# All 64-column products of a pair of experts in one block, all whole-array work in another

## The chip, the cores and the metric

The kernel runs on one core of one Trainium2 chip. The metric is the time of one execution on the device in microseconds (us), the median of several runs.

## What is computed

The kernel is one layer of a decoder trunk for 512 tokens of 1024 features: a norm, four token mixers, an output projection, a second norm, then a mixture of 32 experts of which each token uses two. The change touches the experts alone:

```python
def expert_block(args):
    xe, e = args
    return (jax.nn.silu(xe @ w1[e]) * (xe @ w3[e])) @ w2[e]

yb = lax.map(expert_block, (xb, blk_expert)).reshape(P, D)
yb = yb * row_gate[:, None].astype(yb.dtype)
out = jax.ops.segment_sum(yb, row_tok, num_segments=T + 1)[:T]
```

`w1` and `w3` of an expert are 1024 x 512, `w2` is 512 x 1024, all in float32. The result is multiplied by a vector `g2` and added to `x`.

## The kernel before

Everything up to the router is as before the change and fills the first 819 us. Then the 32 experts are done in 16 pairs. Each expert has 64 slots for its tokens, so a pair has 128; what an expert has beyond 64 tokens is done in a loop of its own, `overflow` (L1396), entered once, at pair 5 (`OVP`).

The work of one pair `p`, and the names that stand for it in the rows:

- `front`: `ph`, the pair's 128 slots against `w1` and `w3`. The two experts' products are 64 columns of the array each and run side by side, so a matrix product there is a tile of 128 x 64. A load brings 512 rows of one matrix; the four parts (two of `w1`, two of `w3`) are 16 instructions each. Then a sigmoid on ScalarE (L1316), a multiplication on VectorE (L1317) and the gating (L1349) give `g`.
- the tables: `pq` (the slots' gates, 4 small products, then L1338 to L1344 on VectorE) and `pr` (four transposes at L1334, copied to `pT` by ScalarE).
- `Back.turn`: four transposes of `g` into `gTp` (L1361), copied to `gT` by ScalarE (L1363).
- `Back.product(n)`: `py`, half `n` of the columns of `gT` times `w2`, again 64 columns of the array per expert, 16 instructions; then `py` times `g2` on VectorE (L1374), `yh` on ScalarE (L158) and `yl` on VectorE (L159), the two parts in which a float32 number goes through the faster product.
- `Back.add(n)`: `po`, `pT` times `yh` and `yl` for each of four blocks of tokens, on the whole array, added to `xm` on VectorE (L1386).
- `group`: every second pair, the rows of 0 and 1 (`pg`, L1097 to L1099 on VectorE) of the next four experts' 256 slots, and `xeps`, 64 whole-array products that gather their tokens, in two halves, one read by ScalarE and one by VectorE (L1480) into `xe`.

All products are issued by `mm` at L60, so one line stands for most of TensorE's work and the names tell it apart. From the router on TensorE's order is the order of the program (a manual schedule); the other engines' order is set by a scheduler.

`front` is a generator that stops behind each of its four parts, and the loop over pairs puts other work into the stops: the additions of the pair before last behind the first and second part, the tables behind the first, `turn` of the pair before behind the third. So 64-column and whole-array products alternate. The second product of pair `p - 1` comes behind `front(p)`. In an odd pair a half of the gather stands ahead of each half of it.

In PSUM `po`, `pr`, `pq` and, up to pair 13, `py` take turns in three buffers of one pool (`psm`); `ph`, `xeps` and the last pairs' `py` take turns in two buffers of twice the size (`psz`). Each half of a product asks for a buffer of its own.

The weights come through SyncE's queue in a fixed list `order`, 198 loads (L1068), into a ring of 18 tiles, each as soon as its tile is free. `w2` of pair `p - 1` stands behind `w1` and `w3` of pair `p` in that list, which is the order of use. At most 76 loads (`most`) are issued ahead of the overflow loop.

Of the kernel before, what the change touches and what calls it, by code (L numbers as in the profile page):

```python
# [39 lines left out]
def trunk(ctx, tc, x, c, ada_w, ada_b, norm1_g, norm2_g, w_in, hgrn_lb, hgrn_norm_g, conv_w, conv_b, conv_ln_g,  # L40
# [7 lines left out]
    def sigmoids(*pairs):  # L48
        """one after the other on ScalarE once all are ready; it otherwise has the table set of exp and ln."""
        with tc.manual_schedule(engines=ACT):  # L50
            if len(pairs) > 1:
                for n, (_, i) in enumerate(pairs):
                    A.activation(tick[:, 2 * n:2 * n + 2], i[:, i.shape[1] - 2:, i.shape[2] - 1] if len(i.shape) == 3 else i[:, 510:512], AF.Copy)
            with tc.high_priority():
                for o, i in pairs:
                    A.activation(o, i, AF.Sigmoid)
                A.preload_act_table_set(LNEXP)
# [20 lines left out]
    # ---- pools of the first part  # L78
# [9 lines left out]
    # ---- loads that everything waits for: c, norm1_g, the first of ada_b; x  # L88
# [7 lines left out]
    # ---- constants  # L96
# [26 lines left out]
    # silu(c) in columns  # L123
# [11 lines left out]
    # ---- x: rms over the row, then transposed  # L135
# [3 lines left out]
    def rsqrt(dst, sums, scale, gain=1.0):  # L139
        """gain / sqrt(sums * scale + EPS), a few columns: exp(-ln / 2) and one Newton step."""  # L140
# [15 lines left out]
    def split(h_ap, l_ap, src):  # L156
        """src = h + l, each of 12 bits."""
        A.activation(h_ap, src, AF.Copy)  # L158
        V.tensor_sub(l_ap, src, h_ap.bitcast(F32))  # L159
# [3 lines left out]
    def ada_load(hf, tiles):  # L163
        """columns hf of 2 of the first two parts of ada_w."""
# [5 lines left out]
    def ada_sum(hf, ps, k):  # L170
        """sh1 and sc1 = silu(c) ada_w (+ ada_b); each quarter on 32 partitions."""
# [12 lines left out]
    def ada_cols(hf, ps):  # L184
        """the sums in columns, into a1 and b1."""
# [40 lines left out]
    def spare(n):  # L226
        """products that nothing needs, so that the array's clock stays up."""
        for _ in range(n):
            mm(scr[:, :128], ident, ident, True, True)
# [12 lines left out]
    # ---- weights: loaded, split in two parts of 12 bits  # L242
# [16 lines left out]
    # ---- the first half of h, the first block's products with it, meanwhile the second half  # L259
# [49 lines left out]
    # ---- masks  # L309
# [29 lines left out]
    def step():  # L339
        """the mixer in hand, as far as its next matrix products; true at its end."""  # L340
# [16 lines left out]
    def three(o, l, r, nk, first=True, last=True):  # L357
        """o += sum over k of (l_h r_h + l_h r_l + l_l r_h); a mixer's products come between."""
# [9 lines left out]
    def fm(w, ci, nk=KD, r=hR):  # L368
        """128 columns of a product, features on partitions."""
# [4 lines left out]
    def tm(w, t, o):  # L374
        """a block's columns of a product, tokens on partitions."""
# [3 lines left out]
    def tm_v(col, nm, tag="d2"):  # L379
        """256 columns, token-major: [128, chunk, 256]."""  # L380
# [22 lines left out]
    def flip(x, nm):  # L403
        """tokens on partitions [128, 4, 256] to features on partitions [128, 2, 512], in PSUM."""
# [6 lines left out]
    def unit(sq, n, gain=1.0):  # L411
        """of squares [128, 1024]: gain / sqrt(mean + EPS) of each n."""
# [6 lines left out]
    # ================= conformer convolution  # L419
# [28 lines left out]
    def conv_ln(res):  # L448
        def over_channels(y, z):
            """a token's sum over the channels / 128, tokens on partitions."""  # L450
# [50 lines left out]
    # ================= HGRN2  # L501
    lbc = mix.tile([128, 4], F32, name="lbc")     # lower bound of the layer: softmax over the layers, cumulated
# [7 lines left out]
    l_a = mix.tile([128, 4], F32, name="l_a")     # max(log(max(lb, 1e-30)), LOG_TINY)  # L510
# [3 lines left out]
    l_c = mix.tile([128, 4], F32, name="l_c")     # log1p(-lb)  # L514
# [20 lines left out]
    def hg_mix(res, hb, f, q, v, g):  # L535
# [22 lines left out]
        # pairs of one position  # L558
# [41 lines left out]
    def linear_out(k, v, am, qd, dec):  # L600
        """o of a linear recurrence, tokens on partitions: in chunks of 128 by am, across them by a state."""
# [29 lines left out]
    def finish(res, o, gcol, hb, g, nm):  # L631
        """head rms, the silu gate; then features on partitions, gain, and split."""
# [17 lines left out]
    # ================= stick breaking  # L650
# [3 lines left out]
    def sb_mix(res, hb, q, k, v):  # L654
# [23 lines left out]
        def scores(p, j):  # L678
            """of a block of 128 keys: log(1 + e^z), and log sigmoid(z); only of the past."""
# [15 lines left out]
        def sums(j, l, lr, start):  # L695
            """et += l sp of a block."""
# [36 lines left out]
    # ================= retention  # L733
# [86 lines left out]
    # ================= the four mixers, the gates and the branch projections  # L820
# [84 lines left out]
    def ada_rest(q, acc_, raws, row=None, before=None):  # L905
        """columns of silu(c) ada_w + ada_b, 1024 of them: on all partitions, or in columns."""
# [31 lines left out]
    def late_sums():  # L938
        """sh2, a2, and g1 once the tables of the retention are done with."""
# [30 lines left out]
    def last_sums():  # L970
        """g1, then g2."""
# [21 lines left out]
    # logits of a token: its x . (a2 wr) over its rms, and sh2 . wr + b  # L993
# [9 lines left out]
    # ================= output projection, second norm, router  # L1003
# [5 lines left out]
    # small tables for the router  # L1009
# [11 lines left out]
    slot = keep.tile([128, 4, NT], F32, name="slot")     # slots and gates of a token's two experts  # L1021
    sg = keep.tile([128, 6, NT], F16, name="sg")         # the same, the gates times 2^15 in two parts of 11 bits
# [7 lines left out]
    # ---- the experts' weights in the order of their use, each tile loaded as soon as there is room  # L1030
# [3 lines left out]
    def cuts(p):  # L1034
        """the columns of a pair's second product, a part at a time; those of the last pair are smaller."""
# [3 lines left out]
    def parts(p, i):  # L1039
        """the rows of a pair's first products, likewise."""  # L1040
# [7 lines left out]
    for p in range(16):  # L1048
# [4 lines left out]
        if 0 < p < 15:  # L1053
            second(p - 1)
        if p > 13:
            second(p)
# [19 lines left out]
    def first_max(v, n, nm, hot=True):  # L1076
        """of v [128, 2, n]: its maxima, the first indices that have them, and those as rows of 0 and 1."""
# [15 lines left out]
    def rows(g, p_, ts):  # L1093
        """the rows of 0 and 1 of 256 slots."""
# [6 lines left out]
    def gather(p_, pv_, ts, ds):  # L1101
        """the slots' tokens, a feature block at a time."""
# [8 lines left out]
    def meanwhile(p_, pv_):  # L1111
        """products for the time in which the second half's experts are found: half of the first gather, in parts,
        and some that nothing needs, so that the array's clock stays up."""
# [19 lines left out]
    def route(half, pl, between=None):  # L1133
        """the experts, ranks in them, and gates of 256 tokens; their rows over their rms, split."""
# [7 lines left out]
        # rows times 2^10, of at most 2^15, in two parts of 11 bits  # L1142
# [43 lines left out]
        # slot of a token in its expert's block of 64; behind that, -1 here  # L1186
# [11 lines left out]
        # gates: softmax of the two, times the group's probability  # L1198
# [71 lines left out]
    def overflow_tables():  # L1270
        """blocks of 128 slots for what an expert has beyond 64 tokens: their number, experts, a token's slot there."""
# [30 lines left out]
    # ================= experts  # L1302
# [4 lines left out]
    def front(p, cur, p_, xe):  # L1307
        """the two experts of a pair: one-hot rows and gates of their slots, silu(x w1) * (x w3) * gate; in parts."""
        so = p % 2 * 128
        ph = psz("ph")  # L1310
        g = None

        def swish():
            nonlocal g
            g = moe.tile([128, 512], F32, name="g", bufs=1)
            A.activation(g, ph[:, 0], AF.Sigmoid)  # L1316
            V.tensor_mul(g, g, ph[:, 0])  # L1317

        for i in range(2):
            if p == 15 and i:  # L1320
                swish()
            for r0, r1 in parts(p, i):
# [5 lines left out]
                yield  # L1328
                if (i, r0) == (0, 512):
                    pr, pq = ps_mm.tile([128, 1024], F16, name="pr", tag="mm"), psm("pq")  # L1330
                    for t in range(NT):
                        mm(pq[:, :6], p_[:, t, so:so + 128], sg[:, :, t], t == 0, t == NT - 1)
                    for t in range(NT):
                        T.transpose(pr[:, t * 128:(t + 1) * 128], p_[:, t, so:so + 128], ident16)  # L1334
                    # the first or the second gate of the token, as it is its first or its second slot
                    ga = moe.tile([128, 4], F32, name="ga")
                    two = pq[:, 2:6].rearrange("p (k a) -> p a k", a=2)
                    V.tensor_scalar(ga[:, 0:1], pid, 128.0 * p, None, op0=OP.add)  # L1338
                    V.tensor_scalar(ga[:, 1:2], pq[:, 0:1], ga[:, 0:1], 2.0 ** -15, op0=OP.is_equal, op1=OP.mult)
                    V.tensor_copy(ga[:, 2:4], two[:, 0])  # L1340
                    V.scalar_tensor_tensor(ga[:, 2:4], two[:, 1], 2.0 ** -11, ga[:, 2:4], op0=OP.mult, op1=OP.add)
                    V.tensor_mul(ga[:, 0:1], ga[:, 1:2], ga[:, 2:3])
                    V.scalar_tensor_tensor(ga[:, 3:4], ga[:, 1:2], 2.0 ** -15, ga[:, 3:4], op0=OP.subtract, op1=OP.mult)
                    V.tensor_sub(ga[:, 0:1], ga[:, 0:1], ga[:, 3:4])  # L1344
                    pT = moe.tile([128, 512], F32R, name="pT")
                    A.activation(pT, pr[:, :512], AF.Copy)
        if p < 15:
            swish()
        V.scalar_tensor_tensor(g, g, ga[:, 0:1], ph[:, 1], op0=OP.mult, op1=OP.mult)  # L1349
        cur[:] = p, g, pT  # L1350

    class Back:
        """a pair's second product, added to its tokens: the parts of the product, then those of the sum."""
# [11 lines left out]
        def product(self, n):  # L1365
            cs = cuts(self.p)[n]
            n_ = cs.stop - cs.start
# [118 lines left out]
    for _ in group(0):  # L1486
        pass
# [68 lines left out]
```

## Time and profile before

| | |
|---|---|
| median of 3 runs | 1319.75 us |
| lowest, highest | 1318.61, 1320.47 us |
| profiled execution: span | 1318.6 us |
| profiled execution: own time | 1318.6 us |
| PE, DVE, ACT busy | 96%, 55%, 35% |
| HBM read, written | 289.68 MB, 2.10 MB |

The span is from the first to the last instruction of the profiled execution. PE is TensorE, PEld its loading of weights, DVE VectorE, ACT ScalarE, SP SyncE. A line number belongs to the kernel before. "128\*64" in a row is the tile of the array. "x16" is the number of instructions in a group or piece. What stands in brackets at the end of a row of the timeline is how long the engine was idle ahead of it, and what it waited for. `PEclk` is the granted clock of TensorE, 1.00 being full speed.

### The profile page before, as it was taken

Reading aid. Unit: us, or ns where it says so; the run is one execution under the profiler, and the core shown is the slowest. Engines: PE = TensorE matmul, PEld = TensorE weight load, DVE = VectorE, ACT = ScalarE, POOL = GpSimd, SP = SyncE. Lnnn points to the kernel's source line nnn. Section 1 sums busy time; section 2 is a strip of 40 time slices with the busy share of each in tenths; the row PEclk is TensorE's granted clock in tenths of the full one; section 3 lists DMA queues with packets and bytes.
Section 4 is the critical chain, followed back from the end, with each engine's and each line's share of the span. In section 5 each row is a group of like instructions: output and inputs, shape, how many; then the busy total and the mean of one; then the engine's idle time right before and its main releaser. Section 6 shows DMA issues by size and latency. Waiting matters only on the chain. (4 is left out here: it accounts for less than half of the span.)

```text
span 1318.6 us, 17997 instructions
## 1 busy us (share of the span) xinstructions
PE 1269.6 (96%) x7265; PEld 881.3 (67%) x7265; DVE 720.7 (55%) x1262; ACT 466.5 (35%) x651; POOL 197.9 (15%) x154
## 2 busy tenths in 40 slices
PE   7999998999999999999999998999989999999997
PEld 5789888987779987787888895444334434343434
DVE  2624679998955464568754565344342444334344
ACT  4447464445454366453334542111101111011111
POOL 3135746101110112121111201000000000000000
PEclk9999997999999999999999998999999999999999
DMA  9422211122222222247782594999989999999997
GB/s 342 140 97 82 79 65 33 50 78 65 96 64 68 94 96 64 81 136 239 248 259 96 196 353 155 385 386 386 387 325 386 387 387 386 387 386 387 386 387 265
DMA packets 177474, 292.98 MB, mean 222 GB/s; under 512 B 8329, under 2 KB 63705, under 8 KB 177389
## 3 DMA queue, kind: packets, MB, share of 16 engines
q1 hardware_dynamic: 174248, 289.45, 61.9%
q10 hardware_dynamic: 2724, 2.26, 0.6%
q8 instruction: 58, 0.95, 0.3%
q14 instruction: 28, 0.22, 0.0%
q0 software_dynamic: 416, 0.10, 0.0%
HBM read 289.68 MB, written 2.10 MB: 221 GB/s over the span
## 5 line engine op out<-in xcount | busy, mean ns | idle before, releaser
L60 PE MATMUL ph<-ew,xe 128*64 128x512 f32 x1024 | 231.8, 597 | 1.4 <-DVE g L1317 1.0
L60 PE MATMUL mm<-hh,wh 128*128 128x512 f32 x448 | 178.9, 399 | 0.0
L60 PE MATMUL mm<-hh,wl 128*128 128x512 f32 x448 | 175.0, 391 | 1.6 <-DVE wl L267 1.6
L255 DVE TENSOR_TENSOR wl<-raw,wh 128x2048 fp32r<-128x2048 f32 x55 | 129.7, 2359 | 83.8 <-ACT wh L254 83.6
L60 PE MATMUL mm<-hl,wh 128*128 128x512 f32 x448 | 174.8, 390 | 0.0
L60 PEld LDWEIGHTS ph<-ew,xe 128*64 128x64 f32 x1024 | 69.5, 137 | 131.3 <-issue 127.8
L254 ACT ACTIVATE wh<-raw 128x2048 fp32r<-128x2048 f32 x55 | 105.2, 1912 | 75.5 <-PE mm L60 75.2
L60 PE MATMUL mm<-wh,hh 128*128 128x256 f32 x448 | 130.4, 291 | 0.0
L60 PE MATMUL mm<-wl,hh 128*128 128x256 f32 x448 | 127.4, 284 | 0.0
L60 PE MATMUL mm<-wh,hl 128*128 128x256 f32 x448 | 127.4, 284 | 0.0
L1386 DVE TENSOR_TENSOR xm<-xm,po 128x512 f32<-128x512 f32 (+1 forms) x136 | 80.4, 651 | 67.7 <-PE po L60 67.7
L60 PE MATMUL py<-ew,gT 128*64 128x512 f32 (+1 forms) x544 | 116.0, 570 | 1.4 <-ACT gT L1363 1.4
L60 PEld LDWEIGHTS mm<-hh,wh 128*128 128x128 f32 x448 | 84.2, 188 | 23.3 <-issue 7.2
L60 PEld LDWEIGHTS mm<-hh,wl 128*128 128x128 f32 x448 | 84.1, 188 | 19.9 <-DVE wl L267 1.9
L60 PEld LDWEIGHTS mm<-hl,wh 128*128 128x128 f32 x448 | 84.2, 188 | 16.6 <-DVE hl L207 0.3
L60 PEld LDWEIGHTS mm<-wh,hh 128*128 128x128 f32 x448 | 86.5, 193 | 6.0 <-issue 5.8
L60 PEld LDWEIGHTS mm<-wl,hh 128*128 128x128 f32 x448 | 86.6, 193 | 0.2
L60 PEld LDWEIGHTS mm<-wh,hl 128*128 128x128 f32 x448 | 86.5, 193 | 0.0
L60 PEld LDWEIGHTS py<-ew,gT 128*64 128x64 f32 x544 | 37.7, 137 | 68.3 <-issue 63.4
L60 PE MATMUL xeps<-pg,xhl 128*128 128x256 f16 x512 | 62.3, 281 | 5.2 <-DVE pg L1099 5.0
L441 DVE SCALAR_TENSOR_TENSOR acc<-z,colB,acc 128x512 f32<-128x512 f32 x90 | 67.2, 789 | 0.0
L60 PEld LDWEIGHTS <-xhl 128*128 128x128 f16 x512 | 50.5, 101 | 23.8 <-issue 16.0
(438 smaller groups left out, 2014.4 us busy)
## 6 DMA issues: line engine op xcount, KB each, us to landing
ew<-in_expert_w_dram SPq DMA_DIRECT2D x186, 1024.0 KB, 14.3
raw<-in_w_in_dram SPq DMA_DIRECT2D x26, 1024.0 KB, 5.0
raw<-in_w_gate_dram SPq DMA_DIRECT2D x16, 1024.0 KB, 5.6
adaw<-in_ada_w_dram SPq DMA_DIRECT2D x64, 256.0 KB, 3.3
aw<-in_ada_w_dram SPq DMA_DIRECT2D x32, 256.0 KB, 5.4
raw<-in_w_branch_dram SPq DMA_DIRECT2D x8, 1024.0 KB, 5.3
raw<-in_w_out_dram SPq DMA_DIRECT2D x6, 1024.0 KB, 6.1
ew<-in_expert_w_dram SPq DMA_DIRECT2D x12, 512.0 KB, 10.0
```

Of the source, the lines that this page charges most:

```text
L60: T.matmul(o, l, r, start=start, stop=stop, skip_group_check=True)
L254: a = A.activation(wh, raw, AF.Copy)
L255: v = V.tensor_sub(wl, raw, wh.bitcast(F32))
L441: V.scalar_tensor_tensor(a, z, cw(k, j), a, op0=OP.mult, op1=OP.add)
L1386: V.tensor_add(xm[:, t, cs], xm[:, t, cs], po)
```

## The change

Three edits, all in the expert phase.

1. `front` is no generator any more. A pair's four parts run one behind the other, `tables` is a function of its own, and the loop over pairs first issues both halves of the second product of the pair before, then all of `front(p)`, and behind it everything on the whole array: the additions, a gather's halves in odd pairs, `turn`, the tables of the next pair. The additions of pair `p - 1` now all come behind `front(p)`; six of the eight stand ahead of `turn` and two behind it. The special order for pairs 14 and 15 is gone.
2. Both halves of a second product of pairs 0 to 14 are one tile `self.py` of the pool with the two large buffers; pair 15 has four parts in tiles of their own as before.
3. The list of loads has `w1`, `w3`, `w2` of each pair, as they are used now.

Comments are gone as well, so line numbers differ.

```diff
-        if 0 < p < 15:
-            second(p - 1)
-        if p > 13:
-            second(p)
+        second(p)
...
-    def front(p, cur, p_, xe):
+    def tables(p, p_):
...
+    def front(p, ga, xe):
         so = p % 2 * 128
         ph = psz("ph")
...
-                yield
-                if (i, r0) == (0, 512):
-                    pr, pq = ps_mm.tile([128, 1024], F16, name="pr", tag="mm"), psm("pq")
...
             cs = cuts(self.p)[n]
+            if self.p < 15 and not n:
+                self.py = psz("py")
             n_ = cs.stop - cs.start
             w = [next(ew), next(ew)]
-            py = (psz("py")[:, 0] if self.p > 13 else psm("py"))[:, :n_]
+            py = psz("py")[:, 0, :n_] if self.p > 14 else self.py[:, n]
...
     for p in range(16):
-        b = Back(*cur) if p else None
-        f = front(p, cur, *gr)
-        gg = group(p // 2 + 1) if p % 2 and p < 15 else iter(())
-        for n, _ in enumerate(f):
-            if b and n == 2 and p < 15:
-                b.turn()
-            if late_ and n < 2:
-                late_.add(0, (2 * n, 2 * n + 1))
-                late_.add(1, (2 * n, 2 * n + 1))
-            if n == 2 and p != OVP:
-                next(gg, None)
+        if b:
+            b.product(0)
+            b.product(1)
+        ga, pT = nxt
+        g = front(p, ga, xe)
         if p == 1:
             eobi, oslot = overflow_tables()
...
+        if p != OVP:
+            next(gg, None)
+        if b:
+            b.add(0)
+        if p != OVP:
+            next(gg, None)
+        if b:
+            b.add(1, (0, 1))
         if p == OVP:
-            for n in range(2):
-                b.product(n)
-            for n in range(2):
-                b.add(n)
+            b.add(1, (2, 3))
             pe_order.close()
...
+        late_, b = b, Back(p, g, pT)
+        b.turn()
+        if late_ and p != OVP:
+            late_.add(1, (2, 3))
...
+        if p < 15:
+            p_, xe = gr
+            nxt = tables(p + 1, p_)
```

How the instructions move, at three places. First TensorE around the second product of an even pair of the later part; `DMAHW..`, `DVE`, `Activation` and `PE` in brackets are the semaphores that an instruction waits for: a load, VectorE, ScalarE, TensorE. Before:

```order
L1361 MATMUL gTp<-ident,g 128x128 x4
L60 MATMUL ph<-ew,xe 64x512 [waits DMAHW5_49]
L60 MATMUL ph<-ew,xe 64x512 [waits DMAHW6_49]
L60 MATMUL ph<-ew,xe 64x512 x6
L60 MATMUL py<-ew,gT 64x512 [waits DMAHW7_49,DVE_49,Activation_49]
L60 MATMUL py<-ew,gT 64x512 [waits DMAHW0_49]
L60 MATMUL py<-ew,gT 64x512 x6
L60 MATMUL py<-ew,gT 64x512 [waits DMAHW1_49,PE_49]
L60 MATMUL py<-ew,gT 64x512 [waits DMAHW2_49]
L60 MATMUL py<-ew,gT 64x512 x6
```

And now:

```order
L60 MATMUL py<-ew,gT 64x512 [waits DMAHW3_49,Activation_49]
L60 MATMUL py<-ew,gT 64x512 [waits DMAHW4_49]
L60 MATMUL py<-ew,gT 64x512 x6
L60 MATMUL py<-ew,gT 64x512 [waits DMAHW5_49,DVE_49]
L60 MATMUL py<-ew,gT 64x512 [waits DMAHW6_49]
L60 MATMUL py<-ew,gT 64x512 x6
L60 MATMUL ph<-ew,xe 64x512 [waits DMAHW7_49,PE_49]
L60 MATMUL ph<-ew,xe 64x512 [waits DMAHW0_49]
L60 MATMUL ph<-ew,xe 64x512 x6
```

`turn` no longer stands between the parts of `ph`; the product comes first and `ph` behind it, and the second half's first product has VectorE among its waits.

Second, TensorE in the whole-array work of an even pair. Before:

```order
L60 MATMUL po<-yh,pT 128x512 [waits DVE_49]
L60 MATMUL po<-yl,pT 128x512
L60 MATMUL ph<-ew,xe 64x512 [waits DMAHW5_49]
L60 MATMUL ph<-ew,xe 64x512 [waits DMAHW6_49]
L60 MATMUL ph<-ew,xe 64x512 x6
L60 MATMUL po<-yh,pT 128x512 [waits DVE_49]
L60 MATMUL po<-yl,pT 128x512
L60 MATMUL po<-yh,pT 128x512 [waits DVE_49]
L60 MATMUL po<-yl,pT 128x512
L60 MATMUL po<-yh,pT 128x512 [waits DVE_49]
L60 MATMUL po<-yl,pT 128x512
```

And now:

```order
L60 MATMUL po<-yh,pT 128x512 [waits DVE_49,Activation_49]
L60 MATMUL po<-yl,pT 128x512
L60 MATMUL po<-yh,pT 128x512 [waits DVE_49]
L60 MATMUL po<-yl,pT 128x512
L1352 MATMUL gTp<-ident,g 128x128 x4
L60 MATMUL po<-yh,pT 128x512 [waits DVE_49]
L60 MATMUL po<-yl,pT 128x512
L60 MATMUL po<-yh,pT 128x512 [waits DVE_49]
L60 MATMUL po<-yl,pT 128x512
L60 LDWEIGHTS pg
L60 MATMUL pq<-sg,pg 128x6 [waits DVE_49]
```

The additions stood in fours on either side of a part of `ph`; now they stand together, with `turn` ahead of the last two and the tables behind them.

Third, VectorE in an even pair, from the gating of `g` to the additions. Before:

```order
L1317 TENSOR_TENSOR g<-g,ph 128x512
L1349 SCALAR_TENSOR_TENSOR g<-g,ga,ph 128x512
L1338 TENSOR_SCALAR ga<-pid 128x1
L1374 TENSOR_TENSOR py<-py,g2b 128x512
L159 TENSOR_TENSOR yl<-py,yh 128x512
L1374 TENSOR_TENSOR py<-py,g2b 128x512
L159 TENSOR_TENSOR yl<-py,yh 128x512
L1386 TENSOR_TENSOR xm<-xm,po 128x512 x8
```

And now, from the split of the product on:

```order
L1367 TENSOR_TENSOR py<-py,g2b 128x512
L159 TENSOR_TENSOR yl<-py,yh 128x512
L1367 TENSOR_TENSOR py<-py,g2b 128x512
L159 TENSOR_TENSOR yl<-py,yh 128x512
L1379 TENSOR_TENSOR xm<-xm,po 128x512
L1339 TENSOR_TENSOR g<-g,ph 128x512
L1379 TENSOR_TENSOR xm<-xm,po 128x512
L1340 SCALAR_TENSOR_TENSOR g<-g,ga,ph 128x512
L1379 TENSOR_TENSOR xm<-xm,po 128x512 x6
L1316 TENSOR_SCALAR ga<-pq,ga 128x1
```

The multiplication and the gating of `g` now stand among the additions, and both halves of the split ahead of all of them.

## Rows read from the trace of the kernel before

**Rows 1.** Page, part 1: busy time, share and instructions of each engine.

```profile
PE 1269.6 (96%) x7265; PEld 881.3 (67%) x7265; DVE 720.7 (55%) x1262; ACT 466.5 (35%) x651; POOL 197.9 (15%) x154
```

**Rows 2.** Stretches: length, busy us of each engine, PEclk, DMA share, GB/s.

```profile
818.90:989.75 170.85, 163.86 (x830) 68.06 (x831) 71.53 (x217) 21.26 (x36) 0.00 (x0) 0.99 0.99 363
989.75:1299.23 309.48, 304.17 (x1554) 131.48 (x1553) 119.09 (x274) 39.50 (x70) 0.00 (x0) 0.99 1.05 385
1299.23:1318.60 19.37, 13.94 (x100) 9.21 (x100) 9.46 (x25) 2.13 (x5) 0.00 (x0) 0.97 0.58 194
```

**Rows 3.** Chain of waits, pairs 6 to 8: start us, us, what.

```profile
1008.96 0.59 PE gTp L1361 x4
...
1020.00 3.43 PE ph L60 x16
1023.44 2.17 PE po L60 x8
1025.60 3.58 PE ph L60 x16
1029.19 0.67 PE po L60 x2
...
1029.88 1.89 DVE xm L1386 x3
...
1031.82 0.38 PE pr L1334 x4
...
1039.96 3.60 PE xeps L60 x32
...
1070.11 0.59 PE gTp L1361 x4
```

**Rows 4.** Timeline, a product's first half: start, us, engine line, out<-in, [idle before].

```profile
1199.82 0.14 PEld L60 LDWEIGHTS py<-ew,gT 128*64 128x64 f32 x2 [0.29 <-issue]
1200.06 0.70 DVE L1374 TENSOR_TENSOR py<-py,g2b 128x512 f32<-128x512 f32 x1 [1.15 <-PE py L60]
...
1200.86 0.60 ACT L158 ACTIVATE yh<-py 128x512 fp32r<-128x512 f32 x1 [3.63 <-DVE py L1374]
...
1201.49 0.69 DVE L159 TENSOR_TENSOR yl<-py,yh 128x512 fp32r<-128x512 f32 x1 [0.72 <-ACT yh L158]
```

**Rows 5.** Timeline of TensorE, pair 15's first products.

```profile
1292.12 2.37 PE L60 MATMUL ph<-ew,xe 128*64 128x512 f32 x10 [1.00 <-DVE g L1317]
```

**Rows 6.** Groups of VectorE, 1000 to 1270 us: count, then busy us, mean ns.

```profile
L1349 DVE SCALAR_TENSOR_TENSOR g<-g,ga,ph 128x512 f32<-128x512 f32 x9 | 6.7, 748 | 0.3
L1317 DVE TENSOR_TENSOR g<-g,ph 128x512 f32<-128x512 f32 x9 | 6.2, 687 | 57.8 <-ACT g L1316 57.8
```

**Rows 7.** Groups of VectorE, 840 to 865 us.

```profile
L1285 DVE TENSOR_SCALAR_CACHE_REDUCE tmp<-ends 128x32 f32<-128x32 f32 x16 | 3.0, 186 | 0.5
```

**Rows 8.** Timeline of VectorE, pair 5's additions; chain of waits behind the overflow loop.

```profile
980.25 3.67 DVE L1386 TENSOR_TENSOR xm<-xm,po 128x512 f32<-128x512 f32 x6
...
989.75 8.18 PE xeps L60 x58
```

**Rows 9.** Chain of waits, the last pair.

```profile
1301.40 3.67 PE py L60 x32
```

**Rows 10.** Timelines of TensorE; then stretches with PEclk third from the end.

```profile
594.95 0.55 PE L794 MATMUL z<-ident,rtk 128*128 128x128 f32 x3 [1.90 <-ACT kt L795]
...
805.60 0.20 PE L60 MATMUL scr<-ident,f1o 128*8 128x2 f32 x2 [1.33 <-DVE f1o L1090]
...
809.20 0.19 PE L60 MATMUL pl<-ohb,trib 128*128 128x32 bf16 x1 [2.43 <-DVE ohb L1178]
...
13.60:17.00 3.40, 3.40 (x22) 2.01 (x24) 0.00 (x0) 3.34 (x6) 0.09 (x1) 0.50 1.05 360
808.90:815.70 6.80, 5.80 (x22) 2.86 (x22) 5.14 (x34) 0.20 (x1) 0.00 (x0) 0.50 0.00 1
590.00:598.00 8.00, 6.10 (x39) 5.24 (x38) 6.67 (x7) 5.41 (x6) 5.16 (x3) 1.00 0.62 189
```

More of the change, by code (lines that the diff above doesn't have):

```diff
@@ L1305, in trunk @@
     ew = stream()
-    def front(p, cur, p_, xe):
+    def tables(p, p_):
+        so = p % 2 * 128
+        pr, pq = ps_mm.tile([128, 1024], F16, name="pr", tag="mm"), psm("pq")
+        for t in range(NT):
+            mm(pq[:, :6], p_[:, t, so:so + 128], sg[:, :, t], t == 0, t == NT - 1)
+        for t in range(NT):
+            T.transpose(pr[:, t * 128:(t + 1) * 128], p_[:, t, so:so + 128], ident16)
+        ga = moe.tile([128, 4], F32, name="ga")
+        two = pq[:, 2:6].rearrange("p (k a) -> p a k", a=2)
+        V.tensor_scalar(ga[:, 0:1], pid, 128.0 * p, None, op0=OP.add)
+        V.tensor_scalar(ga[:, 1:2], pq[:, 0:1], ga[:, 0:1], 2.0 ** -15, op0=OP.is_equal, op1=OP.mult)
+        V.tensor_copy(ga[:, 2:4], two[:, 0])
+        V.scalar_tensor_tensor(ga[:, 2:4], two[:, 1], 2.0 ** -11, ga[:, 2:4], op0=OP.mult, op1=OP.add)
+        V.tensor_mul(ga[:, 0:1], ga[:, 1:2], ga[:, 2:3])
+        V.scalar_tensor_tensor(ga[:, 3:4], ga[:, 1:2], 2.0 ** -15, ga[:, 3:4], op0=OP.subtract, op1=OP.mult)
+        V.tensor_sub(ga[:, 0:1], ga[:, 0:1], ga[:, 3:4])
+        pT = moe.tile([128, 512], F32R, name="pT")
+        A.activation(pT, pr[:, :512], AF.Copy)
+        return ga, pT
+    def front(p, ga, xe):
         so = p % 2 * 128
         ph = psz("ph")
[L1311 to L1317, printed above, removed]
         for i in range(2):
-            if p == 15 and i:
-                swish()
             for r0, r1 in parts(p, i):
@@ L1327, in front @@
                            k == 0, k == KD - 1)
-                yield
-                if (i, r0) == (0, 512):
-                    pr, pq = ps_mm.tile([128, 1024], F16, name="pr", tag="mm"), psm("pq")
[L1331 to L1348, printed above, removed]
+        g = moe.tile([128, 512], F32, name="g", bufs=1)
+        A.activation(g, ph[:, 0], AF.Sigmoid)
+        V.tensor_mul(g, g, ph[:, 0])
         V.scalar_tensor_tensor(g, g, ga[:, 0:1], ph[:, 1], op0=OP.mult, op1=OP.mult)
-        cur[:] = p, g, pT
+        return g
     class Back:
@@ L1483, in group @@
             yield
-    gr, cur, late_ = [], [], None
+    gr = []
     for _ in group(0):
         pass
+    p_, xe = gr
+    nxt, b = tables(0, p_), None
     for p in range(16):
-        b = Back(*cur) if p else None
-        f = front(p, cur, *gr)
-        gg = group(p // 2 + 1) if p % 2 and p < 15 else iter(())
-        for n, _ in enumerate(f):
-            if b and n == 2 and p < 15:
-                b.turn()
-            if late_ and n < 2:
-                late_.add(0, (2 * n, 2 * n + 1))
-                late_.add(1, (2 * n, 2 * n + 1))
-            if n == 2 and p != OVP:
-                next(gg, None)
+        if b:
[3 more added lines that the diff above has]
+        g = front(p, ga, xe)
         if p == 1:
             eobi, oslot = overflow_tables()
-        late_ = b if p < 15 else None
+        gg = group(p // 2 + 1) if p % 2 and p < 15 else iter(())
+        if p != OVP:
[6 more added lines that the diff above has]
+            b.add(1, (0, 1))
         if p == OVP:
-            for n in range(2):
-                b.product(n)
-            for n in range(2):
-                b.add(n)
+            b.add(1, (2, 3))
             pe_order.close()
-            late_, most[0] = None, len(order)
+            most[0] = len(order)
             overflow()
@@ L1512, in trunk @@
             next(gg, None)
-        next(gg, None)
-        if late_ and p < 15:
-            late_.product(0)
-        next(gg, None)
-        if late_ and p < 15:
-            late_.product(1)
-        if p == 14:
-            late_.add(0)
-            late_, c = Back(*cur), late_
-            late_.turn()
-            late_.product(0)
-            c.add(1)
-            late_.product(1)
-    b = Back(*cur)
-    b.turn()
+            next(gg, None)
+        late_, b = b, Back(p, g, pT)
+        b.turn()
+        if late_ and p != OVP:
+            late_.add(1, (2, 3))
+        next(gg, None)
+        if p < 15:
+            p_, xe = gr
+            nxt = tables(p + 1, p_)
     b.product(0)
```

## The prediction

> **What bounds the kernel now.** I read the page's busy shares first, then stretches of the expert phase by engine, then the chain of waits, then single waits. TensorE is busy 96% of the span, VectorE 55% [rows 1]. By stretches TensorE works 163.86 of 170.85 us up to the first gather behind the overflow loop, and 304.17 of 309.48 us from there to the last first product [rows 2]. In the second of these the loads run at 385 GB/s, so a load of 1024 KB takes 2.72 us and the 12 loads of a pair 32.7 us. Two pairs need 65.4 us of transfers, yet TensorE does them in 61.15 us, from one `gTp` of an even pair to the next (1008.96 to 1070.11) [rows 3]. It can, because the loads that ran ahead during the overflow are used up bit by bit. So TensorE sets the pace and the transfers stand close behind: time saved on TensorE is worth only as much as that lead allows, time added to it counts in full.
>
> The chain also prices the pieces. Sixteen 64-column products follow their like in 3.43 us and follow whole-array work in 3.58 us: a change of mode costs about 0.15 us there, and with the slower first `po` some 0.27 us for there and back, an estimate. Four additions take 2.17 us, 32 gathers 3.60, a transpose of `g` 0.59, the tables 0.4 (the 0.38 us piece), an addition on VectorE 0.63 (1.89 for three) [rows 3].
>
> **What the change removes.** A 64-column block now runs uninterrupted, so TensorE changes there and back once a pair instead of some three times in an even pair and five in an odd one: 6 x 0.27 = 1.6 us less per two pairs. Counts of instructions, gathers and bytes stay.
>
> **What it adds: a wait in the middle of each product.** `py` used to be two tiles in separate buffers; now both halves are one tile. The order shows it: the second half's first product waits for VectorE besides its load, where before it waited for none. What it waits for is the last reader of the first half, `yl`. After the last issue of a first half (1199.82) come the multiplication (1200.06, 0.70 us), `yh` on ScalarE (0.60) and `yl` (from 1201.49, 0.69), ending at 1202.18; with 0.06 us to the next engine that is 2.42 us in which TensorE has nothing else, since its order is fixed [rows 4]. Today this chain lies beside the next products. That a write into one half does wait for a reader of the other shows at pair 15, where `ph` stands 1.00 us for the multiplication that reads the other half [rows 5]. So the 64-column block costs 4 x 3.43 + 2 x 3.43 + 2.42 = 23.0 us. The wait's bounds are 0 (no wait) and 2.6 (0.15 us more to restart); I take 2.42.
>
> The Trainium skill, "Perfetto Trace Analysis", section "Optimizing Tensor Performance", says that independent groups should rotate through different PSUM banks so that draining one overlaps the next group's products. By that rule the halves, each with its own columns of the tile, would overlap as before, and the sum would be that of the third rival. The 1.00 us row [rows 5] speaks against it.
>
> **The whole-array block.** Eight additions now stand together, and three buffers let TensorE run ahead by three only. In an even pair VectorE sets the length: the first addition starts 0.69 us in (1029.19 to 1029.88), seven must end before the tables find a buffer (7 x 0.63 = 4.4), between them come the multiplication and gating of `g` (0.69 + 0.75) [rows 3, 6], then 0.4 for the tables: 7.4 us at most, while TensorE's own work is 2 x 2.17 + 0.59 + 0.4 = 5.3. I take 7.2, near the upper end, because each link is an in-order one; both are kept for the range. In an odd pair two gathers of 3.60 us cover VectorE, and TensorE's work decides: 5.3 + 7.2 = 12.5, less 0.1 for one slow first `po`: 12.4. Two pairs thus take 2 x 23.0 + 7.2 + 12.4 = 65.6 us instead of 61.15. Of the 4.45 us, 4.84 is the wait, 1.6 is gained from modes and the rest is VectorE's even block. The transfers need 65.4, so loads wait for nobody and nobody for them: that the order is now w1, w3, w2 costs nothing, as use follows the same order, and SP's queue holds nothing else there.
>
> **The sum**, in three stretches against the profiled execution, whose own time and span are 1318.6 us.
>
> First product to first gather behind the overflow loop, now 170.85 us [rows 2]: 0.4 for the first tables, 13.7 for pair 0's products, 3.6 for turning its `g` with nothing beside it (two passes of ScalarE at 0.60 as that of `yh`, 0.69 + 0.75 on VectorE, 0.59 for the transpose, and crossings) [rows 3, 4, 6]; five blocks of 23.0 (115.0); the whole-array blocks of pairs 1 to 4 (12.4 + 7.2 + 12.4 + 7.2 = 39.2); at pair 1 the tables of the overflow, whose 16 operations of one kind (3.0 us [rows 7]) now stand mostly ahead of the fifth addition, 3.0 (bounds 0, if the gathers cover them, and twice that, with the smaller ones around them); at pair 5 the eight additions, `g` between them, 0.69 + 8 x 0.63 + 1.44 = 7.2; and from the last addition (980.25 + 3.67 = 983.92) to the gather (989.75) 5.8 as now [rows 8]. Together 187.9, which is 17.1 more.
>
> Gather to the end of pair 15's first products, now 309.48 [rows 2]: 64 gathers 8.18 [rows 8], 0.59 and 0.4 for transposes and tables and 0.2 for the changes of mode, 9.4; ten blocks of 23.0; five even whole-array blocks (36.0) and four odd ones (49.6). Together 325.0, 15.5 more.
>
> From there to the end, now 19.37 [rows 2]: pair 14's additions come now between pair 15's `g` and its second product. `gTp` waits for five of them and the gating, so the first `py` starts some 5.9 us behind the last `ph` instead of 2.2 (1299.23, where a stretch of [rows 2] ends, to 1301.40 [rows 9]): 3.8 more. The rest is as before.
>
> So far 1318.6 + 17.1 + 15.5 + 3.8 = 1355.0.
>
> **The clock.** The granted clock was 0.50, the lower of its two levels (1.2 of 2.4 GHz), for 6.8 us from 808.9, where TensorE stood in a 2.43 us wait, with another of 1.33 us shortly ahead of it; behind a lone 1.90 us wait at 593 it stayed at 1.00; the shortest stay at 0.50 in the trace is 3.4 us [rows 10]. The 15 new waits of 2.42 us are as long as the one at 808.9 but with dense work on both sides. None or all falling are the bounds: 0 and 15 x 1.7 (half of 3.4) = 25.5 us, or 51 if each lasted 6.8. I take a third, five falls, 8.5 us: 1363.5. The median of the runs shown, 1319.75, is 1.1 above the profiled execution, so **1364.6** is forecast.
>
> **Rivals**, each worked out as above, 1.1 us for the median included.
> 1. No fall of the clock: 1356.1. For it: dense products on both sides, and the 1.90 us wait that left it up.
> 2. All fifteen fall: 1381.6 at 1.7 each, more if a stay lasts longer, up to 1407.
> 3. No wait between the halves: the first stretch is 12.1 shorter and the gather starts at 994.7. TensorE would then end at 1318.7, but the transfers behind the overflow cannot go faster than now, 328.85 us from gather to end (1318.6 - 989.75), so 1323.6, with the median 1324.7. Against it stands the wait in the order.
> 4. A wait for the first multiplication alone (1.05 us in place of 2.42): 20.5 us less, 1335.6.
> 5. **Faster**: no wait, and the whole-array blocks at TensorE's own 5.3, and overflow tables that hide. The first stretch is 175.8 - 2 x 1.9 - 3.0 - 1.4 = 167.6, the gather starts at 986.5, and with 328.85 behind it 1315.4, on the median 1316.5. The place is the even block at the three buffers; the point is the first stretch under 168.2 us, since 0.2% (2.6 us, about what a measurement of this kernel can tell from no change) of the span must be won there. Every link of VectorE in the trace speaks against it.
> That the change does not do what it says is excluded by the order: one change there and back per pair.
>
> **How the numbers follow.** Some falls, one to about ten: 0.58. Rival 1: 0.26. Rival 2: 0.08. Rivals 3 and 4: 0.03 each. Rival 5: 0.02. The forecast's own range is 1351 (the seven even blocks at 5.3, 1.9 less each) to 1376 (ten falls, 8.5 more, and waits of 2.6, 2.7 more). The range must keep eight in ten and gives up rivals 2 to 5, 0.16: 1349, which is rival 1 with half of the even blocks short, to 1378. Faster by over 0.2%: rival 5, 0.02. Within 0.2%: a third of rival 3, where some other term falls short too, 0.01. Slower: the rest, 0.97.
>
> **What would show it.** Right: TensorE waits on `py` for VectorE's `yl` about 15 times, some 36 us in all; `gTp` of even pairs 65 to 68 us apart; the gather behind the overflow near 1007 to 1010; spells of 0.50 in the clock behind some of the waits; VectorE naming `po` and `pq` waits in even blocks; no wait for loads. Wrong: no wait between the halves, a product's 32 instructions in twice 3.43 us, or waits on loads, which would make the transfers the bound.

## The result, and the profile after

The changed kernel takes 1355.43 us (median of 4 runs, 1352.91 to 1356.53), the kernel before 1319.83 in the same comparison: a ratio of 1.0267, with an interval from 1.0252 to 1.0282. It is slower by 35.6 us. The forecast was 1364.6, with 1349 to 1378 as the range; without its term for the clock it would have been 1356.1.

One entry of the table ahead is wrong. The profiled execution of the changed kernel took 1356.53 us with a span of 1354.6, so 1.9 us lie around the span, and the profiled execution of each experiment shows the same 1.8 to 1.9. The profiled execution of the kernel before will then have been the one of 1320.47 us, not one of 1318.6 as its table says, and stands 0.7 above the median, not 1.1 below it as the prediction has it. The forecast stays as it is: its sum is one of spans, and the 1.1 us that it adds is the median less the span, 1.87 less 0.72. Spans are compared below.

The first part of the page, after; TensorE is busy for 93% instead of 96% [rows 1], for nearly the same time:

```profile
PE 1264.7 (93%) x7265; PEld 883.9 (65%) x7265; DVE 715.5 (53%) x1262; ACT 465.6 (34%) x651; POOL 198.4 (15%) x154
```

The three stretches of [rows 2], after (length, busy us of each engine, PEclk, DMA share, GB/s):

```profile
820.80:1009.03 188.23, 164.60 (x822) 69.37 (x823) 70.02 (x217) 20.89 (x36) 0.00 (x0) 0.97 0.90 329
1009.03:1330.73 321.70, 293.10 (x1539) 130.58 (x1538) 111.23 (x265) 38.36 (x69) 0.00 (x0) 0.99 1.02 376
1330.73:1354.60 23.87, 18.30 (x117) 11.82 (x116) 14.87 (x34) 2.73 (x6) 0.00 (x0) 0.98 0.26 89
```

| stretch | before | forecast | after |
|---|---|---|---|
| up to the first `ph` | 818.90 | 818.90 | 820.80 |
| to the first gather behind the overflow | 170.85 | 187.9 | 188.23 |
| to the end of pair 15's first products | 309.48 | 325.0 | 321.70 |
| to the end | 19.37 | 23.2 | 23.87 |
| span | 1318.6 | 1355.0 | 1354.6 |

"First gather" in the prediction and in this table is a point six gathers in: in the timelines the first begins at 987.91 before and at 1007.19 after, 1.8 us earlier on both sides, so the differences stand.

The 1.9 us of the first line lie ahead of the changed work: the gathers before it begin 1.8 us later too, at 815.76 instead of 813.95. This start differs from run to run, so the runs below are compared by their expert phase as well, from the first `ph` to the end of the span: 499.7 us before, 533.8 after, 34.1 more.

Where TensorE waits from the start of the expert phase on, after, the five largest (us in total, times, longest):

```profile
PE py L60 <- DVE yl L159: 33.6, 15, 2.3
PE po L60 <- DVE xm L1379: 9.4, 19, 0.6
PE xeps L60 <- DVE pg L1096: 5.0, 1, 5.0
PE gTp L1352 <- DVE g L1340: 2.3, 1, 2.3
PE pr L1311 <- DVE xm L1379: 1.5, 7, 0.2
```

The first line is new: 15 waits for `yl`, 2.24 us each. That it is as large as the whole difference is in part chance, since other terms add and take away, as the runs below show. No product waits for a load. The chain of waits over pairs 7 and 8 shows the wait link by link, and the two whole-array blocks (start us, us, what):

```profile
1047.77 3.63 PE py L60 x16
1051.40 0.02 issue
1051.43 0.71 DVE py L1367
...
1052.22 0.61 ACT yh L158
1052.83 0.02 issue
1052.85 0.70 DVE yl L159
1053.55 0.04 issue
1053.60 3.65 PE py L60 x16
1057.25 13.73 PE ph L60 x64
1070.98 2.17 PE po L60 x8
1073.15 3.51 PE xeps L60 x32
1076.66 0.93 PE po L60 x4
1077.59 0.44 PE gTp L1352 x4
1078.03 0.94 PE po L60 x4
1078.97 3.51 PE xeps L60 x32
1082.48 0.08 PE pq L60 x4
1082.56 0.24 PE pr L1311 x4
1082.80 2.29 PE py L60 x9
```

Between the halves TensorE stands from 1051.40 to 1053.60 while the first half is multiplied, copied and subtracted. The 64-column block from 1047.77 to 1070.98 is 23.21 us (forecast 23.0), the odd whole-array block behind it 11.82 (12.4).

### The profile page after: what moved, and what is told of

Same layout as the page of the kernel before. It is cut to its first block, busy times and chain, and to the rows that moved or that the text cites. A ratio compares the mean times of both kernels' runs of the same rounds, so it can differ in the third digit from the quotient of the medians.

```text
span 1354.6 us, 18029 instructions
## 1 busy us (share of the span) xinstructions
PE 1264.7 (93%) x7265; PEld 883.9 (65%) x7265; DVE 715.5 (53%) x1262; ACT 465.6 (34%) x651; POOL 198.4 (15%) x154
## 5 line engine op out<-in xcount | busy, mean ns | idle before, releaser
L60 PE MATMUL ph<-ew,xe 128*64 128x512 f32 x1024 | 222.5, 592 | 0.1
L60 PEld LDWEIGHTS ph<-ew,xe 128*64 128x64 f32 x1024 | 73.5, 137 | 145.9 <-issue 142.5
L60 PE MATMUL py<-ew,gT 128*64 128x512 f32 (+1 forms) x544 | 120.5, 586 | 34.7 <-DVE yl L159 33.6
L60 PEld LDWEIGHTS py<-ew,gT 128*64 128x64 f32 x544 | 36.9, 139 | 106.1 <-issue 53.9
L1338 ACT ACTIVATE g<-ph 128x512 f32<-128x512 f32 x16 | 9.6, 598 | 197.3 <-PE ph L60 197.3
L158 ACT ACTIVATE yh<-py 128x512 fp32r<-128x512 f32 (+1 forms) x34 | 19.4, 572 | 150.1 <-DVE py L1367 150.1
L60 PE MATMUL po<-yh,pT 128*128 128x512 f32 (+1 forms) x136 | 59.2, 438 | 10.3 <-DVE xm L1379 9.4
```

The source lines that it names most:

```text
L60: T.matmul(o, l, r, start=start, stop=stop, skip_group_check=True)
```

## The experiments

Theory: the cost is the wait that one tile for both halves puts between them; the order by itself is worth little either way, since transfers stand close behind TensorE. Rivals: the order itself costs (VectorE's work bunched in whole-array blocks), or the tile's place in its pool.

**One tile per half again.**

```diff
-            if self.p < 15 and not n:
-                self.py = psz("py")
...
-            py = psz("py")[:, 0, :n_] if self.p > 14 else self.py[:, n]
+            py = psz("py")[:, 0, :n_] if self.p > 14 else psm("py")
```

> The changed kernel, with each half of a second product in a tile of its own again (in the pool of three buffers, as before the change). Theory: the 15 waits of about 2.25 us on yl (33.6 us) go and with them the one spell of the lower clock behind such a wait (1.7 us). TensorE alone would then end near 1319, but the gather behind the overflow starts near 996 and the transfers behind it need the 328.85 us that they needed before: about 1325, with waits for loads near the end. Rival: the pace is set by VectorE's work in the whole-array blocks, and the wait only moves to another place (py on the last xm, or po): 1340 to 1355.

1326.59 us, a ratio to before of 1.0047 (1.0029 to 1.0065), where the theory had about 1325; span 1323.9. The waits on `yl` are gone; in the chain a product is one piece again, and TensorE waits for loads three times (waits, then chain):

```profile
PE ph L60 <- DMA ew<-in_expert_w_dram: 4.9, 3, 1.6
```

```profile
1061.14 7.02 PE py L60 x32
1068.16 13.73 PE ph L60 x64
```

The expert phase is 505.8 us (from 818.13). So 28.0 of the 34.1 us hang on the tile. A 64-column block is now 20.75 us instead of 23.21, which is 36.9 less for 15 blocks, but four of the later blocks are 9.3 us longer than that in sum: there products wait for loads, and the loading of weights (PEld) with them, 11.6 us in ten times. The new order without the waits is still 6.1 us behind the kernel before: 3.6 up to the gather behind the overflow (992.57 - 818.13 = 174.44 for 170.85), 2.0 less from there to the end of pair 15's first products (1300.03), and 4.5 more in the tail.

**The shared tile in the old order.** Nothing but the tile is changed in the kernel before.

```diff
-            py = (psz("py")[:, 0] if self.p > 13 else psm("py"))[:, :n_]
+            if self.p < 14 and not n:
+                self.py = psz("py")
+            py = self.py[:, n] if self.p < 14 else psz("py")[:, 0, :n_]
```

> The kernel before, with both halves of a second product of pairs 0 to 13 in one tile as in the changed kernel, and nothing else. Theory: the second half waits for yl wherever it stands right behind the first, at 8 places; where half a gather (3.6 us) stands between, nothing waits. 8 x 2.25 = 18 us: about 1337. Rival: the shared tile costs only together with the new order: 1318 to 1322.

1345.38 us, ratio 1.0195 (1.017 to 1.022); span 1344.2. The rival falls. It is slower than the theory's 1337 by 8, and the profile says why. The waits are as forecast:

```profile
PE py L60 <- DVE yl L159: 17.9, 8, 2.2
```

but behind four of the eight (those that end at 953.17, 984.12, 1157.43 and 1222.73) the granted clock was 0.50 for 3.4 us. The timeline of TensorE at one of them, and the stretches of two (PEclk is the third number from the end):

```profile
953.17 5.35 PE L60 MATMUL py<-ew,gT 128*64 128x512 f32 x16 [2.24 <-DVE yl L159]
```

```profile
953.30:956.70 3.40, 3.40 (x10) 0.96 (x11) 0.00 (x0) 0.00 (x0) 0.00 (x0) 0.50 1.05 388
1158.10:1161.50 3.40, 3.40 (x10) 0.97 (x8) 0.00 (x0) 0.00 (x0) 0.00 (x0) 0.50 1.06 391
```

Sixteen products that take 3.65 us elsewhere take 5.35, so each spell costs 1.7 us: 17.9 + 4 x 1.7 = 24.7. The expert phase is 524.3 us (from 819.88), 24.6 more than before.

**The wait covered instead of removed.** One tile as in the change, but two parts of `ph` between the halves, and the list of loads in that order.

```diff
         for i in range(2):
+            if i and b:
+                b.product(1)
             for r0, r1 in parts(p, i):
...
         if b:
             b.product(0)
-            b.product(1)
```

> The changed kernel with its one tile for both halves, but the first two parts of ph (6.9 us) stand between the two halves of the product, and the list of loads follows that order. Theory: the chain over yl (2.3 us) lies beside ph, so the waits go without any more buffers: as the first kernel, about 1325. Rival: what costs is the tile's place in the pool of two large buffers, not the halves' distance: then more than 1340.

1326.26 us, ratio 1.0048 (1.0029 to 1.0066), expert phase 505.4 (from 820.32): the same as with two tiles, and what the theory had. No line of `yl` is left among TensorE's waits; those for loads sum to 5.3 us in 4 times. The place in the pool is no cause; that nothing stands between the halves is.

**The waits filled.** Products that nothing needs put between the halves, ten calls, then four.

```diff
+            if self.p < 15 and not n:
+                scr = ps_o.tile([128, 512], F32, name="scr", tag="o1")
+                for k in (0, 1, 2, 3, 0):
+                    for j in range(2):
+                        mm(scr[64 * j:64 * j + 64], self.gT[:, k * 128 + 64 * j:k * 128 + 64 * j + 64], w[j][:, k], True, True)
```

> The changed kernel with ten 64-column products that nothing needs put into each of the 15 waits between the halves (2.15 us of the 2.25). Theory: the waits were idle time and stay as long, so the time is that of the changed kernel less the spells of the lower clock behind such waits (1.7 us for each, 0 to 4 in a run): 1351 to 1355, with no spell of 0.50 behind a wait between halves. Rival: the filling delays the multiplication or the second half: 1358 or more.

1384.6 us, ratio 1.0462 (1.0436 to 1.0488). A miss of the edit, not of the wait: each call is two instructions, and the ten took 4.29 us (chain):

```profile
1062.73 4.29 PE scr L60 x20
```

They outlast the wait by 4.29 - 2.24 = 2.05 us, 15 times 30.8, while the second halves no longer restart (3.43 us instead of 3.65, 3.3 in all) and the clock stays up (1.7): 25.8 together, and the expert phase is 25.3 longer (559.1 from 824.05). Hence the second run, with `k in (0, 1)`:

> The changed kernel with four instead of ten products that nothing needs in each of the 15 waits between the halves. Ten took 4.29 us, since each of these calls is two instructions, and so 2.04 us more than the wait that they were to fill; four should take 1.72 us and leave about 0.5 us idle. Theory: the waits are idle time, so the time is that of the changed kernel less one spell of the lower clock in the profiled run (1.7 us): 1351 to 1355, with no spell of 0.50 behind a wait between halves. Rival: products in the wait lengthen it: 1358 or more.

1352.53 us, ratio 1.0242 (1.0216 to 1.0268), within the theory's 1351 to 1355; span 1349.9. What is left of the waits:

```profile
PE py L60 <- DVE yl L159: 7.5, 15, 0.5
```

TensorE's idle time there is down from 33.6 to 7.5 us and the kernel hardly moves: the length of the wait is VectorE's and ScalarE's. The expert phase is 532.2 us (from 817.71), 1.6 less than after the change, and no spell of 0.50 stands behind a wait between halves any more, which is 1.7.

**Loads ahead of the overflow.** With two tiles, 16 and 10 loads instead of 8 may be issued ahead of the loop.

```diff
-OVAHEAD = 8
+OVAHEAD = 16
```

> As the first of these, with 16 instead of 8 loads let ahead of the overflow loop. Theory: the transfers then go on during the overflow and are no bound any more, so the time is TensorE's, 1319 to 1321, and the waits for loads of the first kernel are gone. Rival: TensorE was the bound there too: the same time as that kernel within 0.1%.

1333.88 us, ratio 1.011 (1.0091 to 1.0129): both expectations missed. TensorE's waits name the place:

```profile
PE xeps L60 <- DVE pg L1096: 20.3, 1, 20.3
```

The gather behind the loop came after 20.3 us instead of 5.0 and began at 1006.26 instead of 990.73; from there to the end it is 325.2 us instead of 333.2, and no load is waited for. So the transfers did bind behind the loop, and letting more ahead has its price at the entry, which waited for the issued loads to land: transfers run at over 380 GB/s until about 1003, TensorE and VectorE are idle meanwhile, and VectorE's first work behind the entry begins at 1005.13.

> The changed kernel with a tile per half, and 10 instead of 8 loads let ahead of the overflow loop. With 16 the entry of the loop stood 15 us longer until all of them had landed (TensorE's wait at the gather was 20.3 us), while behind the loop no load was waited for and the rest was 8 us shorter. Theory: a load needs 2.72 us, so two more land just as the additions of pair 5 end; the entry costs nothing more and the 4.9 us of waits for loads go: 1319 to 1322. Rival: any load more is paid for at the entry: 1326 to 1332.

1326.48 us, ratio 1.0032 (1.0017 to 1.0047), the rival's value: nothing gained. The stretches of the two, 8 ahead first, show it (GB/s is the last number):

```profile
982.00:986.00 4.00, 2.70 (x9) 1.19 (x8) 4.00 (x7) 0.00 (x0) 0.00 (x0) 1.00 0.06 21
986.00:990.00 4.00, 0.00 (x0) 0.10 (x1) 1.14 (x6) 0.00 (x0) 0.00 (x0) 0.72 0.21 15
990.00:994.00 4.00, 3.02 (x13) 1.76 (x13) 3.02 (x19) 0.00 (x0) 0.00 (x0) 0.50 0.93 294
```

```profile
982.00:986.00 4.00, 2.98 (x11) 1.38 (x9) 4.00 (x7) 0.00 (x0) 0.00 (x0) 1.00 1.05 389
986.00:990.00 4.00, 0.88 (x4) 0.30 (x2) 1.89 (x4) 0.00 (x0) 0.00 (x0) 0.98 0.56 203
990.00:994.00 4.00, 1.54 (x6) 0.89 (x7) 2.79 (x15) 0.00 (x0) 0.00 (x0) 0.50 0.02 6
```

The two loads more keep the transfers busy some 5 us longer, and they begin again some 5 us later. Ten were too many by little: waits for loads are 4.5 us still.

**The start.** Ten ahead, and the tables of the overflow behind pair 0's work.

```diff
-        if p == 1:
-            eobi, oslot = overflow_tables()
...
+        if not p:
+            eobi, oslot = overflow_tables()
```

> The kernel with a tile per half and 10 loads ahead, and the tables of the overflow put behind pair 0's work in place of pair 1's products, so that VectorE does them beside the 64-column products of pair 1. Theory: they no longer stand ahead of pair 1's additions (the term of 3.0 us), so the overflow is reached 2 to 3 us earlier, and the time is 2 to 3 us under that of the kernel with 10 loads ahead; under 1318, faster than both kernels, if it goes well. Rival: the entry then waits for the ten loads, and nothing is gained.

1326.26 us, ratio 1.0041 (1.0026 to 1.0056): the rival's value again. The wait at the gather is 6.3 us where it was 5.5, so what VectorE gained is partly spent on landing loads, and the transfers take the rest: the expert phase is 504.8 us for 505.1.

**The change of mode priced.** Ten ahead, one useless product of two columns in the middle of `ph`.

```diff
+                if 0 < p < 15 and i and not r0:
+                    mm(ps_o.tile([128, 512], F32, name="scr", tag="o1")[:, :2], ident, ident[:, :2], True, True)
```

> The kernel with a tile per half and 10 loads ahead, with one whole-array product of two columns that nothing needs put into the middle of the 64-column products of pairs 1 to 14: 14 changes of mode there and back more. Theory: 0.27 us each and some 0.05 for the product itself, 4 to 5 us more than the kernel without it. Rival: the changes cost nothing and only the product counts: at most 1.5 us more.

1327.15 us, ratio 1.0039 (1.0022 to 1.0055), 0.7 more than without it and within the scatter of both; the expert phase is 505.6 us for 505.1. In the chain, though, each costs:

```profile
1039.01 6.87 PE ph L60 x32
1045.88 0.31 PE scr L60 x2
1046.19 7.02 PE ph L60 x32
```

14.20 us where `ph` without it is 13.73: 0.47 for there and back with the product itself, 14 times 6.6 us on TensorE. TensorE waits for no load in this run, where the run without it waits 4.5 us: the added work took the place of waits for loads. The median moved as little as the rival said, but not for its reason: a change of mode has a price, and it goes unseen because transfers, not TensorE, bind in the run without it.

**All of it.** Two tiles, 9 ahead, the tables moved, and pair 14's additions between the two matrices of pair 15's first products. The new lines of the last of these:

```diff
+            if i == (p < 15):
+                g = moe.tile([128, 512], F32, name="g", bufs=1)
+                A.activation(g, ph[:, 0], AF.Sigmoid)
+                V.tensor_mul(g, g, ph[:, 0])
+            if not i and p == 15:
+                b.add(0)
+                b.add(1)
```

> A tile per half, 9 loads ahead, the tables of the overflow behind pair 0's work, and pair 14's additions with the sigmoid and multiplication of pair 15 between the two matrices of pair 15's first products, so that they no longer stand ahead of its second product. Theory: with the waits gone the transfers are the bound. From the first load behind the overflow to the end the kernel with 8 ahead took 335.7 us and those with 10 took 329.9, 2.9 less for each load more; the ninth lands about when the additions end, so that it costs nothing at the entry (first load behind the loop near 988), and 2.3 us of the end are to be had: 1318 to 1321 in the median, equal to the kernel before. Rival: TensorE's work still counts in full, and the 2 to 3 us at the start and the 4 at the end give 1315 or less.

1324.2 us against 1323.11 of the kernel before on the same chip, ratio 1.0009 (0.9994 to 1.0024): no difference, as the theory had it; that both lie above the 1318 to 1321 belongs to that comparison, in which the kernel before is 3.3 us slower than in the first. The expert phase is 500.3 us (from 818.10) for 499.7 before, and one wait of 1.0 us for a load is left. No version of the new order beat the kernel before.

## Why the prediction was right, and where its terms were off

- **The wait between the halves** was the main term and the right one: forecast at 2.42 us, 2.24 measured, 15 of 15. Taking the tile apart, sharing it in the old order, covering it and filling it all give what it says. The 1.00 us row of pair 15 [rows 5] was the evidence that counted. Two halves of one tile did not overlap, so rival 3 fell, and rival 4 with it: the wait ends with `yl`, not with the multiplication. The Trainium skill, "Perfetto Trace Analysis", section "Optimizing Tensor Performance", has the draining of one bank overlap the next group's products. The trace of the kernel with a tile per half agrees (a product is one piece of 7.02 us); that of the changed kernel, where both halves are one tile, does not (2.24 us between them).
- **Restarting.** The second half takes 3.65 us behind the wait and the first 3.63 behind whole-array work, where 3.43 was put in; with the shorter wait the block is 23.21 instead of 23.0. The two errors nearly cancel.
- **The whole-array blocks** were put a little too high: the even one is 6.69 us (1041.08 to 1047.77) for 7.2, the odd one 11.82 for 12.4. In the even one VectorE does set the length, as chosen, but its links follow each other in 0.60 to 0.66 us where the mean durations of [rows 6], 0.69 and 0.75, were put in. In the odd one two additions take 0.93 us, where half of the 2.17 for four was used, and a half of the gather 3.51 for 3.60. Over five even and four odd blocks this takes 4.9 us off the second stretch, its start (8.83 us for 9.4) another 0.6, and the ten longer 64-column blocks put 2.1 back: 3.3 us less than forecast.
- **The first stretch** came out as forecast, 188.23 for 187.9, but two spells of the lower clock, some 3.3 us, are in it that stood in another term; without them it is 3.0 shorter than forecast. Of this the tables of the overflow are the largest part: pair 1's whole-array block took 13.38 us (863.13 to 876.51), 1.6 more than another odd one, where 3.0 was put in.
- **The tail** is 4.5 us longer (forecast 3.8): pair 15's second product starts 6.7 us behind its last `ph` (1330.73 to 1337.41), not 5.9.
- **The clock** is the term that was mis-sized: five spells, 8.5 us, of which the profile after shows one behind a wait between halves and one behind the wait for `g` at pair 0:

```profile
838.20:841.60 3.40, 3.22 (x8) 1.00 (x10) 2.76 (x12) 0.62 (x2) 0.00 (x0) 0.50 1.05 387
882.60:886.00 3.40, 3.40 (x10) 0.97 (x10) 0.00 (x0) 0.00 (x0) 0.00 (x0) 0.50 0.99 380
```

  The price, 1.7 us, was right, and the step "I take a third" failed: one in 15 here, four in eight with the shared tile in the old order. So rival 1, no fall at all, came nearest to the time (1356.1), and that is in part luck: the span of 1354.6 holds 1.9 us of later start and 3.3 of two spells, against 5.6 us by which the rest of the sum without the clock (1355.0) was too long. The count also looked at the waits between halves alone. The wait for `g` at pair 0 (2.3 us, then 0.2 to 0.4 ahead of the second product) came with a spell in all ten traces of the new order, the changed kernel's among them, and in neither of the two of the old order, where nothing waits there. How often it happens behind waits of one length is left open; only that it can and what it costs are shown. That the runs of one kernel spread over 3.6 us (1352.91 to 1356.53) would fit it, and the mean granted clock of these runs goes the same way: 0.985 at spans of 1354.6 and 1354.5, 0.986 at 1352.6, 0.987 at 1351.0, where one spell of 3.4 us is worth 0.001. But where the clock fell was seen in one of them only.
- **The transfers**: no load is waited for after the change, as forecast, and with the wait gone two kernels came out at 1326.6 and 1326.3, near the floor of rival 3 (1324.7). Its terms were near too: with a tile per half the gather's point stands at 992.57 for 994.7, and 331.4 us follow it for 328.85.
- **Modes**: 0.27 us for there and back was low; 0.47 with a small product is measured. It decides nothing, since most of what the new order saves on them the even blocks take back, and the transfers the rest: without the waits two pairs take 60.35 us (1028.50 to 1088.85, from one product to the next of even pairs, with a tile per half) instead of 61.15, until loads are waited for.

## What to carry to other kernels

Before products are put back to back, look at which tile each writes and who reads it: a wait that lay beside other work is laid bare when that work is moved away, even if no instruction is added, and two halves of one tile can wait for each other's readers. The remedy is another tile or other products in between; here either took every such wait away and 28 of the 34 us with it. And where two bounds lie within a few per cent, as TensorE's 61 us and the transfers' 65 here, work saved on one is mostly taken by the other; price a gain against the second bound first.

## What the runs showed of the hardware

A wait of 2.24 us between stretches of dense products was followed by 3.4 us of the granted clock at 0.50 in some cases (one of 15 in the changed kernel, four of eight with the shared tile in the old order) and not in the others; sixteen 64-column products took 5.35 us in such a spell instead of 3.65. A single product on the whole array (two instructions), two columns wide, between 64-column products cost 0.47 us. The first load behind the overflow loop followed pair 5's last addition by 1.5 us where the loads had landed (983.92 to 985.39 before), and with 16 loads ahead the wait at the gather grew from 5.0 to 20.3 us.
